# HGRN levels scored in pairs with four level buffers, a resized filler in the last head, and a reordered gate row in the handovers

## The chip, the core and the metric

The kernel runs on one core of one Trainium2 chip. The metric is the device time of one execution in microseconds (us). TensorE (PE in the profile; its weight loads PEld), VectorE (DVE), ScalarE (ACT), GpSimd (POOL) and the DMA queues run side by side, each through its own queue in its own order, and wait for each other by semaphores.

## What is computed

The reference is a two-layer backbone block over 512 latent and 256 context tokens of width 1024, in float32. Layer 0 mixes tokens by retention, layer 1 by a bidirectional gated recurrence (HGRN2) with 8 heads of 128 channels; each layer ends in a gated convolutional feed-forward net (FFN). Around each of the four sub-layers stands the same frame, cut here to its core:

```python
h_l = h_l + g1_l * rms_norm(y_l, norm_g[i, 1])                    # residual, gate row times norm
u_l = rms_norm(h_l, norm_g[i, 2]) * (1.0 + sc2_l) + sh2_l         # input of the next sub-layer
# HGRN2, one head and direction: S_t = diag(a_t) S_{t-1} + k_t v_t^T,  o_t = S_t^T q_t
scores = einsum('bgtk,bgrtsk,bgsk->bgrts', qc, dec, kc)           # dec: product of the gates between s and t
```

## The kernel before

**Order.** TensorE's order is the order in which the program is written (line 1356), except inside the four sub-layer ends, where a small planner writes it. The order on ACT, DVE and POOL is chosen when the program is built, by a scheduler that follows data dependencies, free buffers and its own estimate of times; on the chip each queue is then served in that fixed order.

**HGRN (`hgrn`, from line 1098).** For each head `h`, `project` computes gates `A`, keys `K`, queries and the output gate of the *next* head by large matmuls (tile `hp`, 512 or 256 columns), and `vpart` the values (`hv`). `attend` (line 1168) does the recurrence of the present head in blocks of 128 tokens. Inside a block it doubles the span level by level: for level `li` (0 to 6), ACT copies half of `K` and POOL half of `Q` into a buffer `L` (lines 1201, 1202; three buffers), then DVE multiplies the other halves of `K` and `Q` by the gate totals of this level (line 1208). TensorE forms the scores of the level by `hl`, eight products of 128 x 64 by 128 x 64 (line 1215; sixteen records in the profile), into a PSUM tile of `sml`, of which there are two, and DVE places them by mask into `DG` (line 1219, two instructions). A diagonal `hd` (line 1188), of the same form, stands ahead of level 0. Then follow transposes `ht`, states `hc` and `S`, the output `ho` and its norm `hn`.

**Weaving.** `attend` gives up the floor at every `yield n`. `weave` (line 1285) then lets the filler generator run until it has issued `quota * acc / 37` matmul columns, `acc` being the sum of the yields so far. For heads 0 to 6 the filler is the projection of the next head. For head 7 it is `out1` (line 1266): eight outputs of four chunks, a chunk being three matmuls of 512 columns (`hwo`), which is 8 x 4 x 1536 = 49152 columns, and one step of a side task (`ada`) counted as 4096. Its quota is 64000.

**Sub-layer ends (`tail`, line 515; `handover`, line 392).** A sub-layer's last product is cut into parts of one 128-token block and 512 columns (`tl`). `norms` adds to the plan for each block: two DVE additions out of PSUM (L421), two ACT squares (L424), the factor (L428, L142 to L144), two DVE products of the result with the gate row (L439), one DVE instruction that multiplies by the factor and adds the residual (L450) and the store of the new residual by POOL's DMA queue, then ACT squares (L452), a second factor and the scaling by it, half on DVE (L457), half on ACT (L459). `turn` transposes pairs of blocks on TensorE (L473), modulates (L482) and splits them (L489, L490) into the `u` that the next sub-layer's first products `ld` read. The planner (`Plan.run`, line 49) steps a clock with the costs written in the code; of the ready steps of an engine it emits the one of lowest rank. Transposes have rank 0, the `ld` pieces (24 matmuls each) rank 2, and a transpose counts as ready 0.8 us after its last input. Names of the sub-layer ends: `m0` and `e0` (six blocks, layer 0), `m1` (four blocks, after HGRN), `e1` (the end of the kernel, which has no next sub-layer).

Of the kernel before, what the change touches and what calls it, by code (L numbers as in the profile page):

```python
# [13 lines left out]
ALU = mybir.AluOpType  # L14

P = 128
D = 1024
NF = 8
TL = 512
# [19 lines left out]
class Plan:  # L39
# [5 lines left out]
    def add(self, eng, cost, deps, rank, emit, slack=0.0):  # L45
        self.steps.append(Step(eng, cost, list(deps), rank, emit, slack))
        return self.steps[-1]
# [22 lines left out]
class Net:  # L70
# [321 lines left out]
    def handover(self, nm, y, hsrc, gain, mods, u, hdst, nb, big, tmp):  # L392
        nc = self.nc
        per = y[0].shape[1]
        hx = [big([P, 3, D], F32, f"hx{nm}{j}") for j in range((nb + 2) // 3)]
        if nb % 3:
            g = hx[-1][:, 2:3]
        else:
            g = big([P, 3, D], F32, "gr" + nm)[:, 0:2]
        small = lambda n, w: self.cp.tile([P, w], F32, tag=f"sm{w}", name=f"{n}{nm}", bufs=12)  # L400
        rows = hsrc.rearrange("(b p) d -> p b d", p=P)
        for j, x in enumerate(hx):
            n = min(3, nb - 3 * j)
# [3 lines left out]
        yb = lambda b: y[b // per][:, b % per]  # L407
        hb = lambda b: hx[b // 3][:, b % 3]
# [3 lines left out]
        def norms(b, tails):  # L412
            ts, v, pr = slice(b * P, b * P + P), int(b >= 4), b // 2
            ss, r, q = {}, {}, {}
            add = self.plan.add
            half = lambda c: slice(c * 512, c * 512 + 512)

            def evac(c):
                if not c:
                    ss[0] = small(f"ss{b}", 4)  # L420
                nc.vector.tensor_tensor(yb(b)[:, half(c)], tails[c].ps, yb(b)[:, half(c)], ALU.add)  # L421

            def square(c):
                nc.scalar.activation(tmp(f"sq{nm}{b}{c}"), yb(b)[:, half(c)], AF.Square, accum_out=ss[0][:, c : c + 1])  # L424

            def start(d, x):
                d[0] = small(f"{'rq'[d is q]}{b}", 2)
                nc.scalar.activation(d[0][:, 0:1], x, AF.Abs_reciprocal_sqrt, bias=self.eps, scale=1.0 / D)  # L428

            sq = []  # L430
            for c in range(2):
                e = add("DVE", 0.67, [tails[c]], (pr, 0), lambda c=c: evac(c))
                tails[c].freed = e
                sq.append(add("ACT", 0.75, [e], (pr, 1), lambda c=c: square(c)))
            n = add("DVE", 0.16, sq, (-1,), lambda: nc.vector.tensor_tensor(ss[0][:, 2:3], ss[0][:, 0:1], ss[0][:, 1:2],
                                                                            ALU.add))
            n = add("ACT", 0.28, [n], (-1,), lambda: start(r, ss[0][:, 2:3]))
            n = add("DVE", 0.55, [n], (-1,), lambda: self.newton(r[0], ss[0][:, 2:3]))
            yg = [add("DVE", 0.69, [sq[c]], (pr, 1), lambda cs=half(c): nc.vector.tensor_tensor(  # L439
                yb(b)[:, cs], yb(b)[:, cs], g[:, v, cs], ALU.mult)) for c in range(2)]  # L440
            if u is None:
                for c in range(2):
                    cs = half(c)
                    n = add("DVE", 0.75, [n, yg[c]], (pr, 2), lambda cs=cs: (
                        nc.vector.scalar_tensor_tensor(hb(b)[:, cs], yb(b)[:, cs], r[0][:, 0:1], hb(b)[:, cs],
                                                       ALU.mult, ALU.add),
                        nc.sync.dma_start(hdst[ts, cs], hb(b)[:, cs])))
                return None
            n = add("DVE", 1.28, [n, *yg], (pr, 2), lambda: (
                nc.vector.scalar_tensor_tensor(hb(b), yb(b), r[0][:, 0:1], hb(b), ALU.mult, ALU.add),  # L450
                nc.gpsimd.dma_start(hdst[ts], hb(b))))
            n = add("ACT", 1.23, [n], (pr, 3), lambda: nc.scalar.activation(yb(b), hb(b), AF.Square,  # L452
                                                                           accum_out=ss[0][:, 3:4]))
            n = add("ACT", 0.28, [n], (-1,), lambda: start(q, ss[0][:, 3:4]))
            n = add("DVE", 0.55, [n], (-1,), lambda: self.newton(q[0], ss[0][:, 3:4]))

            return [add("DVE", 0.65, [n], (pr, 3), lambda: nc.vector.tensor_scalar(  # L457
                        yb(b)[:, half(0)], hb(b)[:, half(0)], q[0][:, 0:1], None, ALU.mult)),
                    add("ACT", 0.65, [n], (pr, 3), lambda: nc.scalar.activation(  # L459
                        yb(b)[:, half(1)], hb(b)[:, half(1)], AF.Copy, scale=q[0][:, 0:1]))]  # L460
# [640 lines left out]
    def hgrn(self, outs0, u, mk, nxt):  # L1101
        nc, t, tc = self.nc, self.t, self.tc
# [5 lines left out]
        ip = ies.enter_context(tc.tile_pool(name="heads", bufs=1))  # L1108
        tl = lambda shape, tag, name, bufs: ip.tile(shape, F32, tag=tag, name=name, bufs=bufs)
        tmp = lambda n, w=TL: hp.tile([P, TL], F32, tag="t", name=n, bufs=8)[:, :w]  # L1110
        mf = tl([P, 7, P], "L", "mf", 3)
        nc.scalar.dma_start(mf, t["masks"])
        masks = hp.tile([P, 7, P], U8, name="masks")
        nc.vector.tensor_copy(masks, mf)
        ident = self.ident
        half = lambda n: hp.tile([P, 4, TL], F32, tag="og", name=n, bufs=2)
        og = [half(f"hog{j}") for j in range(2)]
        y, gh, vs = [], [], {}
        ck = lambda x, n: x[:, n * P : n * P + P]
        n4 = lambda x: x.rearrange("p (n l) -> p n l", l=P)  # L1120
# [47 lines left out]
        def attend(h, z):  # L1168
            A, K, q, g = z["A"], z["K"], z["q"], z["g"]
            v = lambda n: vs[h - h % 2][1][n][:, (h % 2) * P : (h % 2) * P + P]  # L1170
            k0 = tmp(f"k0{h}")
# [4 lines left out]
            for li in range(7):  # L1176
# [3 lines left out]
                nc.gpsimd.tensor_tensor(nt, pr[:, :, :, 0], pr[:, :, :, 1], ALU.mult)  # L1180
                tots.append(nt)
                cur = nt
            yield 4
            ps = self.sml(f"hd{h}")
            for n in range(4):
                for b in range(2):
                    rows = slice(64 * b, 64 * b + 64)
                    nc.tensor.matmul(ck(ps, n)[rows, rows], ck(k0, n)[:, rows], ck(q, n)[:, rows],
                                     start=True, stop=True, tile_position=(0, 64 * b))
            DG = tl([P, 4, P], "DG", f"DG{h}", 1)  # L1190
            for b in range(2):
                rows = slice(64 * b, 64 * b + 64)
                nc.vector.tensor_tensor(DG[rows, :, rows], n4(ps)[rows, :, rows],
                                        ident[rows, rows].unsqueeze(1).broadcast_to([64, 4, 64]), ALU.mult)
            for li in range(7):
                hh = 1 << li
                vw = lambda x: x.rearrange("p (n l) -> p n l", l=2 * hh)
                hf = (slice(0, hh), slice(hh, 2 * hh))
                L = tl([P, 2, TL], "L", f"L{h}{li}", 3)
                for d in range(2):  # L1200
                    nc.scalar.activation(vw(L[:, 0])[:, :, hf[d]], vw(K[:, d, LAT])[:, :, hf[d]], AF.Copy)
                    nc.gpsimd.tensor_scalar(vw(L[:, 1])[:, :, hf[1 - d]], vw(Q[:, d])[:, :, hf[1 - d]], 1.0, 0.0,  # L1202
                                            ALU.mult, ALU.add)
                tt = tots[li].rearrange("p d (n l) -> p d n l", l=2)
                for X, d, hd in ((K, 0, 0), (K, 1, 1), (Q, 0, 1), (Q, 1, 0)):
                    nb = X.shape[2] // (2 * hh)
                    xv = vw(X[:, d])[:, :, hf[hd]]
                    nc.vector.tensor_tensor(xv, xv, tt[:, d, :nb, 1 - hd : 2 - hd].broadcast_to([P, nb, hh]), ALU.mult)
                yield 3
                ps = self.sml(f"hl{h}{li}")  # L1210
                x = int(li == 6)
                for n in range(4):
                    for b in range(2):
                        rows, cols = (slice(64 * z, 64 * z + 64) for z in (b, b ^ x))
                        nc.tensor.matmul(ck(ps, n)[rows, cols], ck(L[:, 0], n)[:, rows], ck(L[:, 1], n)[:, cols],  # L1215
                                         start=True, stop=True, tile_position=(0, 64 * b))
                for b in range(2):
                    rows, cols = (slice(64 * z, 64 * z + 64) for z in (b, b ^ x))
                    nc.vector.copy_predicated(DG[rows, :, cols],
                                              masks[rows, li, cols].unsqueeze(1).broadcast_to([64, 4, 64]),  # L1220
                                              n4(ps)[rows, :, cols])
            tot = tots[7]
            order = ((4, 5, 0, 1, 2, 3), (5, 4, 3, 2, 1, 0))
            KT = tl([P, 2, 5, P], "KT", f"KT{h}", 1)
# [76 lines left out]
        z = {}  # L1301
        for _ in chain(project(0, z, outs0), vpart(0, range(3))):
            pass
        for h in range(NF):
            zn = {}
            if h == 7:
                work, quota = out1(), 64000
            elif h % 2:
                work = project(h + 1, zn, None, vpart(h + 1, range(3)))
                quota = 83000  # L1310
            else:
                work = project(h + 1, zn, None, vpart(h, range(3, 6)))
                quota = 83000
            weave(attend(h, z), quota, 37, work)
            z = zn
# [118 lines left out]
```

## Time and profile before

| | us |
|---|---|
| median of 3 runs | 2145.89 (2145.05 to 2146.91) |
| profiled execution, its own time | 2144.12 |
| span of the profiled execution | 2142.4 |

The span starts with the first instruction of the program and ends with the last. Retention fills the span to about 679 us, the first FFN from there to about 1253, HGRN from about 1288 to 1731, the second FFN the rest; the sub-layer ends lie between. A row of a timeline gives start, duration, engine, line, operation, output and inputs, shapes and the number of merged instructions, and in brackets the engine's idle time ahead of it with what ended it. A matmul's printed duration holds its latency, so starts, not durations, tell its rate.

### The profile page before, as it was taken

The numbers are of one execution on the slowest core, as the hardware profiler recorded it, in microseconds if no ns is written. First come the engines' busy times: TensorE is split into PE (matmuls) and PEld (weight loads), VectorE is DVE, ScalarE is ACT, GpSimd is POOL, SyncE is SP. The second block draws the span as 40 slices with busy tenths as digits, with TensorE's granted clock in tenths as the row PEclk, the third lists the DMA queues.
The fourth block names the chain that finished last, engine by engine and source line by source line (L and its number), as shares of the span: only waits on it lengthen the run. The fifth ranks groups of instructions, "written<-read, shape, count | busy, mean of one in ns | idle before, by whom it ended". The sixth has DMA issues, their size and how long they took to land.

```text
span 2142.4 us, 30771 instructions
## 1 busy us (share of the span) xinstructions
PE 2098.6 (98%) x12288; PEld 1770.1 (83%) x12288; DVE 1344.5 (63%) x2560; ACT 839.4 (39%) x1623; POOL 287.8 (13%) x367
## 2 busy tenths in 40 slices
PE   6999999999999999999999999999999989999998
PEld 4888888888888988788888889888888778888886
DVE  6866565663623677477677566778787864434445
ACT  5542342423613733323122147444444454333323
POOL 3622040220100000000000002333333200000000
PEclk9999999999999999999999999999999989999999
DMA  9122313234133233333333533212121243322233
GB/s 301 40 79 87 120 40 128 79 98 149 50 108 118 91 118 99 119 119 109 128 100 127 188 99 108 60 41 60 40 60 41 79 158 131 99 99 97 85 101 120
DMA packets 186608, 218.24 MB, mean 102 GB/s; under 512 B 6112, under 2 KB 157664, under 8 KB 185696
## 3 DMA queue, kind: packets, MB, share of 16 engines
q1 hardware_dynamic: 180432, 198.90, 28.6%
q0 software_dynamic: 2736, 13.11, 1.6%
q10 hardware_dynamic: 3296, 4.26, 0.6%
q8 instruction: 97, 1.59, 0.3%
q14 instruction: 47, 0.39, 0.1%
HBM read 200.90 MB, written 15.34 MB: 101 GB/s over the span
## 4 chain that ended last, share of the span: by engine, by line
PE 92%; DVE 4%; ACT 2%; DMA 1%; issue 0%; POOL 0%; SPq 0%; DVEq 0%
PE f L121 26%; PE f L1059 12%; PE hp L121 8%; PE v L817 6%; PE tl L526 5%; PE wo L985 5%; PE ld L121 4%; PE g_l L121 4%; PE av L868 3%; PE hv L121 3%; PE qk_l L121 3%; PE g_c L121 2%; PE s L121 2%; PE hl L1215 2%; PE qk_c L121 2%; PE hwo L121 1%
## 5 line engine op out<-in xcount | busy, mean ns | idle before, releaser
L121 PE MATMUL f<-um,hua 128*128 128x512 f32 (+1 forms) x960 | 258.3, 357 | 0.0
L121 PE MATMUL f<-um,huv 128*128 128x512 f32 (+1 forms) x960 | 255.8, 354 | 0.0
L264 DVE SCALAR_TENSOR_TENSOR rows<-rada,sc,rows 128x256 f32<-128x256 f32 x504 | 231.8, 485 | 5.4
L1059 PE MATMUL f<-hd,gt 128*128 128x512 f32 x720 | 228.2, 396 | 0.0
L121 PEld LDWEIGHTS f<-um,hua 128*128 128x128 f32 x960 | 169.5, 189 | 29.7 <-issue 4.4
L121 PEld LDWEIGHTS f<-um,huv 128*128 128x128 f32 x960 | 170.0, 189 | 25.2
L121 PE MATMUL hp<-ue,hhw 128*128 128x512 f32 (+1 forms) x672 | 190.8, 371 | 0.0
L121 PE MATMUL f<-um,lua 128*128 128x512 f32 (+1 forms) x480 | 170.1, 354 | 0.0
L121 PE MATMUL f<-um,luv 128*128 128x512 f32 (+1 forms) x480 | 169.7, 354 | 0.0
L1059 PEld LDWEIGHTS f<-hd,gt 128*128 128x128 f32 x720 | 134.9, 187 | 33.6 <-issue 0.8
L1059 PE MATMUL f<-ld,gt 128*128 128x512 f32 x360 | 142.2, 395 | 0.0
L121 PEld LDWEIGHTS hp<-ue,hhw 128*128 128x128 f32 x672 | 113.0, 189 | 17.5 <-issue 1.4
L121 PE MATMUL hp<-ue,lhw 128*128 128x512 f32 (+1 forms) x336 | 120.2, 358 | 0.4
L817 PE MATMUL v<-hv,ua 128*128 128x512 f32 x384 | 120.5, 390 | 0.0
L121 PEld LDWEIGHTS f<-um,lua 128*128 128x128 f32 x480 | 90.7, 189 | 13.0
L121 PEld LDWEIGHTS f<-um,luv 128*128 128x128 f32 x480 | 90.7, 189 | 12.7
L1031 DVE TENSOR_TENSOR c<-f,c 128x512 f32<-128x512 f32 (+1 forms) x60 | 36.1, 602 | 98.3 <-PE f L121 98.3
L1202 POOL TENSOR_SCALAR L<-Q 128x256 f32<-128x256 f32 x112 | 59.6, 545 | 221.3 <-DVE Q L1174 125.2
L985 PE MATMUL wo<-hwo,ogr 128*128 128x512 f32 x288 | 89.3, 391 | 0.0
L1018 ACT ACTIVATE c<-f,c_conv_b,c_conv_w 128x512 f32<-128x512 f32 (+1 forms) x60 | 42.1, 703 | 113.9 <-PE f L121 113.9
L817 PEld LDWEIGHTS v<-hv,ua 128*128 128x128 f32 x384 | 72.1, 188 | 15.4 <-issue 0.6
L93 ACT ACTIVATE hua<-rua 128x512 fp32r<-128x512 f32 x80 | 44.2, 620 | 100.4 <-DMA rua<-ffn_w_up 53.9
(502 smaller groups left out, 4753.3 us busy)
## 6 DMA issues: line engine op xcount, KB each, us to landing
rada<-ada_w SPq DMA_DIRECT2D x48, 1024.0 KB
rua<-ffn_w_up SPq DMA_DIRECT2D x20, 1024.0 KB
ruv<-ffn_w_up SPq DMA_DIRECT2D x20, 1024.0 KB
rd<-ffn_w_down SPq DMA_DIRECT2D x24, 768.0 KB
rhw<-hg_w_in SPq DMA_DIRECT2D x28, 512.0 KB
rv<-ret_w_in SPq DMA_DIRECT2D x8, 1024.0 KB
rg<-ret_w_in SPq DMA_DIRECT2D x8, 1024.0 KB
rqk<-ret_w_in SPq DMA_DIRECT2D x6, 1024.0 KB
```

The source lines that it names most:

```text
L93: self.nc.scalar.activation(hi, raw, AF.Copy)
L121: nc.tensor.matmul(o, a, b[:, s], start=(i == 0), stop=(i == n - 1))
L264: nc.vector.scalar_tensor_tensor(rows[:, v], raw[:, k], a, rows[:, v], ALU.mult, ALU.add)
L526: self.nc.tensor.matmul(step.ps, l, r[:, k], start=(k == 0 and z == 0), stop=(k == 3 and z == 2))
L817: nc.tensor.matmul(ps, a, b, start=(c == 0 and k == 0 and z == 0), stop=(c == 1 and k == 3 and z == 2))
L868: nc.tensor.matmul(av[width][d], a[:, s, ds], b, start=(first and z == 0), stop=(last and z == 2))
L985: nc.tensor.matmul(ps, l, r[:, k], start=(h == 0 and k == 0 and z == 0), stop=(h == 2 and k == 3 and z == 2))
L1018: nc.scalar.activation(c[:, s], ps, AF.Identity, bias=cb[:, i, mt : mt + 1], scale=w(1))
L1031: nc.vector.tensor_tensor(c[:, s], ps, c[:, s], ALU.mult)
L1059: nc.tensor.matmul(ps, l, r[:, k], start=(k1 + k == 0 and z == 0), stop=(k1 + k == nt - 1 and z == 2))
L1202: nc.gpsimd.tensor_scalar(vw(L[:, 1])[:, :, hf[1 - d]], vw(Q[:, d])[:, :, hf[1 - d]], 1.0, 0.0, ALU.mult, ALU.add)
L1215: nc.tensor.matmul(ck(ps, n)[rows, cols], ck(L[:, 0], n)[:, rows], ck(L[:, 1], n)[:, cols], start=True, stop=True, tile_position=(0, 64 * b))
```

## The change

Three edits.

1. **Levels in pairs.** `attend` is cut into `prepare` (buffer, copies, multiplications), `cells` (the eight products) and `place`. Level 0 is prepared ahead of the first yield, which becomes 7, and its products follow those of the diagonal directly. Levels 1 and 2, 3 and 4, 5 and 6 are prepared together, then one `yield 6`, then the products of both, then both placements. The level buffers become four.
2. **Filler of head 7.** Its quota becomes 53248 (49152 + 4096).
3. **Gate row.** In the three sub-layer ends that have a successor, the two products with the gate row (0.69 each in the plan) are gone; the factor and the gate row are applied in one instruction (1.28), and a separate addition of the residual (1.23) follows, with the store behind it. `e1` keeps its form.

```diff
-            yg = [add("DVE", 0.69, [sq[c]], (pr, 1), lambda cs=half(c): nc.vector.tensor_tensor(
-                yb(b)[:, cs], yb(b)[:, cs], g[:, v, cs], ALU.mult)) for c in range(2)]
             if u is None:
+                yg = [add("DVE", 0.69, [sq[c]], (pr, 1), lambda cs=half(c): nc.vector.tensor_tensor(
+                    yb(b)[:, cs], yb(b)[:, cs], g[:, v, cs], ALU.mult)) for c in range(2)]
...
-            n = add("DVE", 1.28, [n, *yg], (pr, 2), lambda: (
-                nc.vector.scalar_tensor_tensor(hb(b), yb(b), r[0][:, 0:1], hb(b), ALU.mult, ALU.add),
-                nc.gpsimd.dma_start(hdst[ts], hb(b))))
+            n = add("DVE", 1.28, [n], (pr, 2), lambda: nc.vector.scalar_tensor_tensor(
+                yb(b), yb(b), r[0][:, 0:1], g[:, v], ALU.mult, ALU.mult))
+            n = add("DVE", 1.23, [n], (pr, 2), lambda: (
+                nc.vector.tensor_tensor(hb(b), hb(b), yb(b), ALU.add), nc.gpsimd.dma_start(hdst[ts], hb(b))))
...
-        mf = tl([P, 7, P], "L", "mf", 3)
+        mf = tl([P, 7, P], "L", "mf", 4)
...
-            yield 4
-            ps = self.sml(f"hd{h}")
...
-            for li in range(7):
+            def prepare(li):
...
-                L = tl([P, 2, TL], "L", f"L{h}{li}", 3)
+                L = tl([P, 2, TL], "L", f"L{h}{li}", 4)
...
-                yield 3
+                return L
+
+            def cells(li, L):
                 ps = self.sml(f"hl{h}{li}")
...
+                return li, ps
+
+            def place(li, ps):
...
+            L = prepare(0)
+            yield 7
+            ps = self.sml(f"hd{h}")
...
+            done = cells(0, L)
...
+            place(*done)
+            for l0 in (1, 3, 5):
+                Ls = [prepare(li) for li in (l0, l0 + 1)]
+                yield 6
+                for done in [cells(l0 + z, Ls[z]) for z in range(2)]:
+                    place(*done)
...
             if h == 7:
-                work, quota = out1(), 64000
+                work, quota = out1(), 53248
```

## Rows read from the trace of the kernel before

**Rows 1.** The page, parts 1 and 4: TensorE's share; the chain by engine.
```profile
PE 2098.6 (98%) x12288; PEld 1770.1 (83%) x12288; DVE 1344.5 (63%) x2560; ACT 839.4 (39%) x1623; POOL 287.8 (13%) x367
...
PE 92%; DVE 4%; ACT 2%; DMA 1%; issue 0%; POOL 0%; SPq 0%; DVEq 0%
```

**Rows 2.** TensorE's timeline around level 0 of head 0; last two rows: later windows.
```profile
1339.90 0.40 PE L121 MATMUL hp<-ue,hhw 128*128 128x256 f32 x2
1340.14 0.28 PE L121 MATMUL hp<-ue,lhw 128*128 128x256 f32 x1
1340.35 0.69 PE L1215 MATMUL hl<-L 128*64 128x64 f32 x16
...
1341.31 0.28 PE L121 MATMUL hp<-ue,lhw 128*128 128x256 f32 x1
...
1340.46 0.58 PE L1215 MATMUL hl<-L 128*64 128x64 f32 x14
...
1340.81 0.23 PE L1215 MATMUL hl<-L 128*64 128x64 f32 x2
```

**Rows 3.** TensorE's timeline around the states `hc`, heads 2 and 7.
```profile
1470.77 0.39 PE L121 MATMUL hp<-ue,lhw 128*128 128x512 f32 x1
1471.00 1.05 PE L1238 MATMUL hc<-hv,KT 128*128 128x128 f32 x8
...
1472.35 0.39 PE L121 MATMUL hp<-ue,lhw 128*128 128x512 f32 x1
1472.58 0.62 PE L121 MATMUL hp<-ue,hhw 128*128 128x512 f32 x2
...
1719.23 1.95 PE L1238 MATMUL hc<-hv,KT 128*128 128x128 f32 x16
```

**Rows 4.** Timeline of head 3: ACT's copies for level 1, and its products.
```profile
1489.40 0.91 ACT L1201 ACTIVATE L<-AK 128x256 f32<-128x256 f32 x2 [3.28 <-DVE AK L1208]
...
1494.70 0.69 PE L1215 MATMUL hl<-L 128*64 128x64 f32 x16
```

**Rows 5.** Timeline of head 1: levels 4 and 6 on TensorE, DVE between them.
```profile
1405.94 0.69 PE L1215 MATMUL hl<-L 128*64 128x64 f32 x16
...
1414.00 0.69 PE L1215 MATMUL hl<-L 128*64 128x64 f32 x16
...
1407.30 5.03 DVE L94 TENSOR_TENSOR lhw<-rhw,hhw 128x512 fp32r<-128x512 f32 x4
1412.36 1.88 DVE L1219 COPY_PREDICATED DG<-masks,hl 64x256 f32<-64x256 uint8 x4
```

**Rows 6.** Head 7, by stretch (start:end, length, busy, PEclk); longest waits; the side task.
```profile
1687.26:1692.69 5.43, 2.97 (x26) 2.19 (x26) 5.38 (x12) 2.44 (x5) 0.81 (x2) 1.00 0.56 193
1692.69:1713.92 21.23, 21.23 (x173) 15.64 (x173) 20.70 (x43) 9.15 (x21) 4.52 (x8) 0.92 0.16 51
1713.92:1730.55 16.63, 12.20 (x88) 10.74 (x85) 6.56 (x17) 5.23 (x10) 0.00 (x0) 0.90 0.41 130
...
PE hc L1238 <- DVE S L1246: 3.3, 1, 3.3
PE hl L1215 <- DVE DG L1193: 2.5, 1, 2.5
...
1712.91 1.07 PE L216 MATMUL ada<-rada,sc 128*32 128x256 f32 x16
```

**Rows 7.** Timeline of the end `m0`: the last block on DVE, its transposes, `ld`.
```profile
729.30 1.28 DVE L450 SCALAR_TENSOR_TENSOR hxm<-yr,r5m,hxm 128x1024 f32<-128x1024 f32 x1
...
732.70 0.49 DVE L457 TENSOR_SCALAR yr<-hxm,q5m 128x512 f32<-128x512 f32 x1
...
734.66 1.04 PE L473 MATMUL trm<-c_ident,yr 128*128 128x128 f32 x8
...
742.27 0.38 PE L121 MATMUL ld<-um,hfl 128*128 128x256 f32 x1 [0.34 <-DVE um L490]
```

**Rows 8.** Timeline of the end `m1`: ACT, first pair of blocks.
```profile
1748.78 2.20 ACT L583 ACTIVATE hfl<-rfl 128x512 fp32r<-128x512 f32 x4 [2.71 <-PE tl L526]
1750.88 1.04 ACT L452 ACTIVATE yh<-hxm 128x1024 f32<-128x1024 f32 x1
```

More of the change, by code (lines that the diff above doesn't have):

```diff
@@ L1182, in attend @@
                 cur = nt
-            yield 4
-            ps = self.sml(f"hd{h}")
[L1185 to L1189, printed above, removed]
-            DG = tl([P, 4, P], "DG", f"DG{h}", 1)
[L1191 to L1194, printed above, removed]
-            for li in range(7):
+            DG = tl([P, 4, P], "DG", f"DG{h}", 1)
+            def prepare(li):
                 hh = 1 << li
@@ L1216, in attend @@
                                          start=True, stop=True, tile_position=(0, 64 * b))
+                return li, ps
+            def place(li, ps):
+                x = int(li == 6)
                 for b in range(2):
@@ L1221, in attend @@
                                               n4(ps)[rows, :, cols])
+            L = prepare(0)
+            yield 7
+            ps = self.sml(f"hd{h}")
+            for n in range(4):
+                for b in range(2):
+                    rows = slice(64 * b, 64 * b + 64)
+                    nc.tensor.matmul(ck(ps, n)[rows, rows], ck(k0, n)[:, rows], ck(q, n)[:, rows],
+                                     start=True, stop=True, tile_position=(0, 64 * b))
+            done = cells(0, L)
+            for b in range(2):
+                rows = slice(64 * b, 64 * b + 64)
+                nc.vector.tensor_tensor(DG[rows, :, rows], n4(ps)[rows, :, rows],
+                                        ident[rows, rows].unsqueeze(1).broadcast_to([64, 4, 64]), ALU.mult)
+            place(*done)
[4 more added lines that the diff above has]
+                    place(*done)
             tot = tots[7]
```

## Prediction

> **What bounds the kernel now.** I read the page first. TensorE is busy for 98% of the span and carries 92% of the chain that ended last [rows 1]. The reader is to see there that only what shortens TensorE's own queue, or its waits, can move the time; work taken from DVE, ACT or POOL counts only where TensorE waits for it. Then I read TensorE's waits by stretch. In heads 0 to 6 of HGRN they are next to nothing. In head 7 they are large: two of them make 5.8 us [rows 6]. In the sub-layer ends there are a few us each. So edit 1 has to be priced as TensorE's own work in heads 0 to 6, edit 2 as waits in head 7, and edit 3 as waits in `m0`, `e0` and `m1`. Last I read the timelines of these places.
>
> **Edit 1: what a group of small products costs.** Take level 0 of head 0 [rows 2]. The 256-column matmuls around it start 0.12 us apart (1339.90 to 1340.14 for two). The one at 1341.31 is the third after that of 1340.14, so without the group it would have started at 1340.14 + 3 x 0.12 = 1340.50. The group costs 1341.31 - 1340.50 = 0.81 us. Inside it twelve of the sixteen records start between 1340.46 and 1340.81, which is 0.029 us each, so sixteen are worth 0.47. The other 0.81 - 0.47 = 0.34 us are paid once per group, in getting in and out. Is that the price of any group, or of this form? The states `hc` answer: sixteen of them start 0.11 us apart ((1.95 - 0.28)/15, with about 0.28 for the latency of the last). Eight between matmuls of 512 columns, which start 0.23 apart, push the third matmul from 1470.77 + 0.69 = 1471.46 to 1472.35, by 0.89 = 8 x 0.11 [rows 3]. They pay nothing for the change. So the 0.34 belongs to the products of 64 columns, and two such groups in a row should pay it once.
>
> The Trainium skill, "TensorEngine Tiling (Array Packing)", Key Properties, says that changing the tiling mode drains the engine while changing the tile does not; that is the reading which the two rows favour. Against the edit speaks "TensorE: Matmul & The Clock Gate" of the Trainium skill, section "Back-to-back issue gap": with hardware decode off a matmul of 64 columns or fewer costs about 62 ns of issue, and a merged group would then save nothing. Sixteen at 62 ns would be 0.99 us, more than the 0.81 that the whole group takes here, so that condition does not hold in this trace. With the floor of about 25 ns that the same section gives, the estimate for the part paid once would be 0.41 instead of 0.34.
>
> Each of the 8 heads has seven levels and a diagonal, 8 such groups. They become 4 per head. Heads 0 to 6 thus lose 7 x 4 = 28 changes: 28 x 0.34 = **-9.5 us**, wholly on TensorE's path.
>
> **What edit 1 makes TensorE wait for.** Two things must now be ready together, the level buffers and both `sml` tiles. Buffers: level 1 of head 3 has the smallest margin of heads 0 to 6, copies done at 1490.31 for products at 1494.70, 4.4 us [rows 4]. With four buffers nothing is prepared later, and in columns of filler no level but the first of a pair moves, and that one later. I price this at nothing, under cover of those 4.4 us. PSUM: level 6 needs the tile that level 4's placement frees, level 5 that of level 3. In head 1 DVE does 5.03 us of weight splitting ahead of the placements, and four placements, 1.88 us, end at 1414.24 against level 6 at 1414.00; the first two of them, level 4's, end at 1413.3 [rows 5]. Between the end of level 4 and level 6 lie 1414.00 - 1405.94 - 0.62 = 7.4 us, and without level 5 between them 6.6. If DVE keeps the splitting ahead of both placements of a pair, it needs 5.03 + 1.88 and some 0.8 of multiplications, 7.7 us, 1.1 more than there is; level 5's own 0.47 runs in that time, and TensorE would wait about 0.6 us. If it doesn't, nothing. With all multiplications of the next pair ahead as well (eight, some 3.9 us) it would be 10.8 and the wait 4 us. The rows are nearest to the middle case, with the splitting ahead of one placement only and 0.7 us to spare (1414.00 against 1413.3). I take 0.1 per head, **+0.7**, with bounds 0 and +28 (7 x 4).
>
> **Edit 2, head 7.** By the quotas, before: 8 chunks stand ahead of level 0, and 28 chunks and `ada` ahead of level 6; the filler is used up two steps later, and the states run bare. After: 7 chunks ahead of the first group, then 6, 5 and 6, so 24 ahead of levels 5 and 6; then 1, 1 and 2 ahead of the three transposes, `ada` and no chunk ahead of the first state, 0, 1, 1, 2 for the rest. Four chunks (4 x 3 x 0.23 = 2.7 us) and `ada` (1.07, about 1 us of the stream) move behind level 6. DVE is full in the first two stretches (5.38 of 5.43, 20.70 of 21.23) and idle for more than half of the third (6.56 of 16.63) [rows 6]. So up to level 6 TensorE only waits in place of the chunks that left: the gain there is at most the 1 us of `ada` that stood directly ahead of it. In the third stretch the moved 3.7 us fill the waits, 16.63 - 12.20 = 4.4 us; the 3.3 at `hc` also falls because no weights can be split on DVE between the states now (their buffer comes free with the last chunk). PEclk of 0.90 over 16.63 us means some 3.3 us at the lower level, 1.2 GHz, after TensorE's wait; that is 1.7 us of work, lost or not as the new waits fall. The same late split is a new load in `m1`'s start: four ACT splits (2.20 together [rows 8]) and four on DVE beside the last head's norm, up to 1 us. Sum: -1 (before level 6) - 1.7 (clock) - 0.3 (rest of the waits) + 0.5 = **-2.5**, bounds -6 (all 5.8 us of waits gone) and 0.
>
> **Edit 3, the sub-layer ends.** On DVE a block gives up two gate products of 512 columns and gains one addition of 1024. The trace has no such addition there; the nearest row is L450 with 1.28 [rows 7], of the same width and with two tensors from SBUF, and I take 1.2. Total work is about even, but the products ran beside the squares, and the addition stands in the chain: +1.2 us for a block whose chain ends last. In `m0` that is the last block: its half scaled on DVE is done at 733.19, the transposes start at 734.66 [rows 7], 1.47 later, at the end of an `ld` piece. So +1.2 is covered by 0.3 if the order on TensorE stays. But the planner calls the transposes ready 0.8 after their input, so by its rule the margin is 0.67, below 1.2, and they would go behind the next piece (24 x 0.12 = 2.9 us). Then the pieces left cannot cover the second half of the chain, and `ld` at 742.27 comes about 2 us later (2.9 less what ACT makes up by running all four modulations back to back). `e0` shows the same pattern with the same 1.47. I take the later place at two in three: **+1.35 each, +2.7**, bounds 0 and +2.9 each. In `m1` ACT is idle for 2.7 us ahead of 1748.78 and the squares of the first block come only behind four splits, at 1750.88 [rows 8]. Without gate products DVE reaches that block's residual earlier, so that its squares fit into the idle time: **-0.3**, bounds -1 and +1. The store of the residual and its POOL queue shift by 1.2 us and nobody waits for that.
>
> **Sum.** -9.5 + 0.7 - 2.5 + 2.7 - 0.3 = -8.9. The profiled execution took 2144.12 (span 2142.4), so 2135.2 there; the median stands 1.8 above it, so **2137.0**.
>
> **The rivals.**
> - *Everything hides (A+).* The transposes keep their place, head 7 gains 6: -9.5 - 6 - 0.3 gives 2130. For it: 0.3 us of margin, and 5.8 us of waits. Against: the planner's 0.8, DVE full in head 7.
> - *Pairs wait for PSUM, mildly.* The 0.6 us computed above in every head: 7 x 0.6 - 0.7 = +3.5 on the forecast, and with the late place fully paid 2.6 more: 2140.5 to 2143. For it: rows 5. Against: the placements are older in the program than the splitting.
> - *Slower: pairs wait for PSUM, badly.* The scheduler puts the weight splitting and the multiplications of the next pair ahead of four placements, and TensorE waits 2 us or more per head. It decides from 4 x 0.34 = 1.36 us per head on; at 2.0 it is 14.0, and -8.9 - 0.7 + 14.0 = +4.4 gives 2150.3, at 2.5 it gives 2154. For it: DVE is the fullest engine beside TensorE [rows 1]. Against: in the rows the placements still came in time.
> - *The merge saves nothing.* The 0.34 is then paid per tile of PSUM or per semaphore, not per change of form: +9.5, 2145 to 2147. Against: the states, eight or sixteen, pay nothing [rows 3].
>
> **How the numbers follow.** About 0.2% (4.3 us) is what a measurement of this kernel can tell from no change: faster means below 2141.6, slower above 2150.2. Forecast 0.70, with 2132 to 2141; A+ 0.07; mild waiting 0.11, half of it below 2141.6; no saving 0.07; slower 0.05. Faster 0.70 + 0.07 + 0.05 = 0.82; same 0.06 + 0.07 = 0.13; slower 0.05. For 8 in 10 the range holds the forecast, part of mild waiting and the near end of A+: 2131 to 2142.
>
> **What would show it.** Right: 28 changes fewer, merged groups of 32 records that take about 1.28 us out of the stream where two took 1.62; heads 0 to 6 some 9 us shorter together; TensorE's wait at `hc` in head 7 under 1 us; a longer wait of `ld` at the ends of `m0` and `e0`. Wrong: waits of `hl` or `ht` on L1219 in heads 0 to 6, or a merged group with a hole between its halves; transposes at the old place with no wait; a head 7 that waits at level 5 for longer than the waits that it lost.

## The result, and the profile after

The changed kernel takes 2131.77 us (2128.56 to 2131.78, median of 4 runs) against 2146.07 (2145.05 to 2146.91, 4 runs) on the same chip: ratio 0.9932, 95% interval 0.9918 to 0.9945. The profiled execution took 2131.78, span 2130.1, against a span of 2142.4 before: 12.3 us less in the profile, where the medians give 14.3. By the page TensorE still bounds the kernel, as in [rows 1]; DVE has 6% of the chain instead of 4%.

```profile
PE 2089.7 (98%) x12288; PEld 1769.8 (83%) x12288; DVE 1337.4 (63%) x2544; ACT 837.5 (39%) x1623; POOL 295.2 (14%) x367
...
PE 91%; DVE 6%; ACT 2%; DMA 1%; issue 0%; POOL 0%; SPq 0%; DVEq 0%; ACTq 0%
```

Where the 12.3 us went shows the view of busy time by stretch: start and end, length, busy time of PE, PEld, DVE, ACT and POOL with instructions, the granted clock of TensorE, DMA share, GB/s. The five rows are `m0`, `e0`, heads 0 to 6, head 7 and `m1`, each from TensorE's first to its last matmul of the part. Between `m0` and `e0` and behind `m1` the two kernels agree within 0.1. Before:

```profile
678.35:752.21 73.86, 72.83 (x480) 66.67 (x479) 51.44 (x112) 51.18 (x111) 3.26 (x6) 1.00 0.34 123
1252.77:1323.40 70.63, 68.09 (x432) 61.01 (x432) 49.55 (x109) 52.34 (x114) 3.20 (x6) 1.00 0.34 112
1323.40:1682.20 358.80, 358.00 (x2873) 308.48 (x2872) 279.97 (x508) 154.39 (x323) 129.42 (x177) 1.00 0.19 54
1682.20:1730.55 48.35, 40.87 (x299) 31.58 (x298) 37.18 (x76) 21.86 (x43) 9.12 (x15) 0.93 0.28 89
1730.55:1790.64 60.09, 55.92 (x337) 48.71 (x336) 40.04 (x83) 37.59 (x80) 2.20 (x4) 0.91 0.38 133
```

After:

```profile
677.45:749.83 72.38, 72.38 (x481) 66.60 (x480) 50.99 (x106) 52.12 (x113) 3.25 (x6) 1.00 0.36 128
1250.37:1317.95 67.58, 67.58 (x432) 60.90 (x432) 49.34 (x104) 51.93 (x114) 3.19 (x6) 1.00 0.32 106
1317.95:1670.54 352.59, 351.04 (x2874) 307.60 (x2873) 274.61 (x507) 153.75 (x323) 137.19 (x177) 1.00 0.20 57
1670.54:1716.72 46.18, 40.05 (x299) 31.41 (x298) 34.37 (x72) 19.51 (x39) 9.00 (x15) 0.93 0.22 72
1716.72:1778.30 61.58, 55.77 (x338) 48.97 (x336) 40.68 (x81) 39.46 (x85) 2.20 (x4) 0.89 0.41 145
```

Length minus PE's busy time is PE's waiting. In `m0` and `e0` it falls to nothing (73.86 - 72.83 = 1.0 and 2.5 before), and these parts are 1.5 and 3.1 shorter. Heads 0 to 6 are 6.2 us shorter, but their waiting rises from 0.8 to 1.6. Head 7 is 2.2 shorter, `m1` is 1.5 longer (waiting 4.2, then 5.8). The stretch ahead of `m0`, which no edit touches, is 0.9 shorter; over all profiles here it lies between 0.9 under and 2.95 over that of before, and with it goes TensorE's granted clock there, in shares of 2.4 GHz: 0.993 before, 0.995 after, 0.988 in the longest (e8 below). So the edits are judged by stretch, and the medians only say whether the sum agrees.

**The merged group.** TensorE's timeline in head 0, levels 3 and 4, answers to [rows 2]:

```profile
1348.58 0.28 PE L121 MATMUL hv<-lhv,ue 128*128 128x256 f32 x1
1348.70 0.28 PE L121 MATMUL hv<-hhv,ue 128*128 128x256 f32 x1
1348.91 1.15 PE L1208 MATMUL hl<-L 128*64 128x64 f32 x32
1349.99 0.39 PE L121 MATMUL hv<-hhv,ue 128*128 128x256 f32 x1
1350.21 0.28 PE L121 MATMUL hv<-lhv,ue 128*128 128x256 f32 x1
```

The matmul at 1350.21 is the second after that of 1348.70 and would have stood at 1348.94: the 32 records cost 1.27 us. Two groups of 16 cost 2 x 0.81 = 1.62 before. The switch that is saved, the way into the 64-column form and out of it, is worth the 0.34 of the prediction within 0.01. The same reckoning over all groups of heads 0 to 6 gives 45.9 us for the 56 of before and 39.1 for the 28 of after, of which 28 x 1.274 = 35.7 are the products and 3.4 are waits inside or at the edge of a group (0.7 before).

**The waits of the pairs** lie between the two halves. Timelines of ACT, TensorE and DVE in head 2 (levels 1 and 2), then of TensorE and DVE in head 3 (diagonal and level 0):

```profile
1435.15 0.42 ACT L1192 ACTIVATE L<-AK 128x256 f32<-128x256 f32 x1 [0.38 <-DVE AK L1199]
...
1439.25 0.69 PE L1208 MATMUL hl<-L 128*64 128x64 f32 x16
1440.20 0.69 PE L1208 MATMUL hl<-L 128*64 128x64 f32 x16 [0.26 <-ACT L L1192]
...
1439.60 0.46 DVE L1216 COPY_PREDICATED DG<-masks,hl 64x256 f32<-64x256 uint8 x1
...
1481.46 0.69 PE L1226 MATMUL hd<-qg,k 128*64 128x64 f32 x16
1482.26 0.69 PE L1208 MATMUL hl<-L 128*64 128x64 f32 x16
...
1481.53 0.68 DVE L143 SCALAR_TENSOR_TENSOR whg<-hn,whg 128x512 f32<-128x512 f32 x1
```

The releaser printed for 1440.20 is an ACT copy. But ACT's two copies for level 2 had, by their order, ended by 1435.6 (first row); what ends at 1440.06 is the placement of level 0 on DVE, which still reads the small PSUM tile that level 2 needs. In head 3 level 0 starts after DVE has read `hn`, the tile of the norm of the head before. And the last pair of head 2 meets the case of [rows 5]: DVE has the weight splitting ahead, the four placements begin at 1453.77, and the group at 1455.17 has a hole that makes it 1.40 long instead of 1.15:

```profile
1455.17 1.40 PE L1208 MATMUL hl<-L 128*64 128x64 f32 x32
...
1451.52 2.22 DVE L94 TENSOR_TENSOR lhw<-rhw,hhw 128x512 fp32r<-128x512 f32 x2
1453.77 1.88 DVE L1216 COPY_PREDICATED DG<-masks,hl 64x256 f32<-64x256 uint8 x4
```

**Head 7**, TensorE's waits there (line waiting, releaser, sum, times, longest), answers to [rows 6]: the 3.3 at the states is gone, the wait behind the diagonal has grown from 2.5 to 4.0.

```profile
PE hl L1208 <- DVE DG L1231: 4.0, 1, 4.0
PE hl L1208 <- DVE DG L1216: 1.6, 1, 1.6
```

**The sub-layer ends.** Timelines of `m0`, blocks 4 and 5. The first three rows are DVE and ACT before, then DVE, ACT, DVE and PE after (they answer to [rows 7]):

```profile
712.99 0.69 DVE L421 TENSOR_TENSOR yr<-tl,yr 128x512 f32<-128x512 f32 x1 [0.17 <-PE tl L526]
...
722.92 1.94 ACT L482 ACTIVATE hxm<-trm,mod,mv0A 128x256 f32<-128x256 f32 x4 [0.58 <-PE trm L473]
...
725.77 0.64 ACT L424 ACTIVATE sqm<-yr 128x512 f32<-128x512 f32 x1
```
```profile
717.51 0.68 DVE L421 TENSOR_TENSOR yr<-tl,yr 128x512 f32<-128x512 f32 x1
...
718.63 0.61 ACT L424 ACTIVATE sqm<-yr 128x512 f32<-128x512 f32 x1
...
719.25 0.55 ACT L483 ACTIVATE hxm<-trm,mod,mv0A 128x256 f32<-128x256 f32 x1
...
723.47 1.28 DVE L449 SCALAR_TENSOR_TENSOR yr<-yr,r5m,grm 128x1024 f32<-128x1024 f32 x1
724.78 1.23 DVE L452 TENSOR_TENSOR hxm<-hxm,yr 128x1024 f32<-128x1024 f32 x1
...
728.85 0.48 DVE L458 TENSOR_SCALAR yr<-hxm,q5m 128x512 f32<-128x512 f32 x1
...
730.95 1.03 PE L474 MATMUL trm<-c_ident,yr 128*128 128x128 f32 x8
```

The addition takes 1.23 us and stands in the chain, as forecast. But the chain starts earlier: before, the squares of the last block stood on ACT behind the whole modulation of the pair before it (725.77); now they are done ahead of it (718.63). Before, nothing on DVE kept them back: the last addition out of PSUM for these two blocks ended at 713.68, 12 us ahead of them. They were late by the order in which ACT's queue was written; inside the ends the planner's order holds for ACT and DVE too, not only for TensorE (`manual_schedule` in `tail`). The block is scaled at 729.3 instead of 733.2, and its transposes stand one `ld` piece earlier, not later.

In `m1` it went the other way ([rows 8]): DVE puts four weight splits between the scaling and the addition of block 1, its squares come at 1741.45, and the first transposes wait 4.58 us.

```profile
1736.39 2.50 DVE L588 TENSOR_TENSOR lfl<-rfl,hfl 128x512 fp32r<-128x512 f32 x4
1738.81 1.22 DVE L452 TENSOR_TENSOR hxm<-hxm,yh 128x1024 f32<-128x1024 f32 x1
...
1741.45 1.04 ACT L453 ACTIVATE yh<-hxm 128x1024 f32<-128x1024 f32 x1
...
1745.45 1.73 PE L474 MATMUL trm<-c_ident,yh 128*128 128x128 f32 x7 [4.58 <-DVE ss3m L435]
```

### The profile page after: what moved, and what is told of

It is laid out like the page before. It is cut to its first block, busy times and chain, and to the rows that moved or that the text cites. A ratio compares the mean times of both kernels' runs of the same rounds, so it can differ in the third digit from the quotient of the medians.

```text
span 2130.1 us, 30763 instructions
## 1 busy us (share of the span) xinstructions
PE 2089.7 (98%) x12288; PEld 1769.8 (83%) x12288; DVE 1337.4 (63%) x2544; ACT 837.5 (39%) x1623; POOL 295.2 (14%) x367
## 4 chain that ended last, share of the span: by engine, by line
PE 91%; DVE 6%; ACT 2%; DMA 1%; issue 0%; POOL 0%; SPq 0%; DVEq 0%; ACTq 0%
PE f L121 26%; PE f L1060 12%; PE hp L121 6%; PE v L818 6%; PE tl L527 5%; PE ld L121 5%; PE wo L986 5%; PE g_l L121 4%; PE av L869 4%; PE hv L121 3%; PE qk_l L121 3%; PE g_c L121 2%; PE s L121 2%; PE qk_c L121 2%; PE hl L1208 1%; PE hc L1255 1%
## 5 line engine op out<-in xcount | busy, mean ns | idle before, releaser
L1193 POOL TENSOR_SCALAR L<-Q 128x256 f32<-128x256 f32 x112 | 67.6, 615 | 211.6 <-DVE Q L1175 130.8
L818 PEld LDWEIGHTS v<-hv,ua 128*128 128x128 f32 x384 | 72.1, 188 | 15.3 <-issue 0.6
```

The source lines that it names most:

```text
L818: nc.tensor.matmul(ps, a, b, start=(c == 0 and k == 0 and z == 0), stop=(c == 1 and k == 3 and z == 2))
```

## The experiments

All lengths in us, from the profile of each kernel by the same five stretches; in brackets what TensorE waits in it. The medians are beside the kernel before of the same session, which took 2145.2 (first eight), 2144.1 (the next two) and 2144.7 (the last two).

| kernel | median | ratio, 95% interval | `m0` | `e0` | heads 0-6 | head 7 | `m1` |
|---|---|---|---|---|---|---|---|
| before | | | 73.9 (1.0) | 70.6 (2.5) | 358.8 (0.8) | 48.4 (7.5) | 60.1 (4.2) |
| after | 2131.8 | 0.9918-0.9945 | 72.4 (0) | 67.6 (0) | 352.6 (1.6) | 46.2 (6.1) | 61.6 (5.8) |
| e1 edit 3 alone | 2141.6 | 0.9974-0.9991 | 72.4 (0) | 67.6 (0) | 358.8 (0.8) | 48.9 (9.3) | 60.9 (5.8) |
| e2 edit 1 alone | 2140.2 | 0.9962-0.9982 | 73.9 (1.0) | 72.1 (2.5) | 352.5 (1.6) | 48.7 (9.0) | 57.5 (4.2) |
| e3 edit 2 alone | 2142.3 | 0.9975-0.9993 | 73.9 (1.0) | 70.6 (2.5) | 358.8 (0.8) | 46.5 (5.3) | 59.4 (4.6) |
| e4 one tile | 2128.1 | 0.9910-0.9935 | 72.4 (0) | 67.6 (0) | 348.3 (0.3) | 45.1 (6.5) | 60.8 (5.8) |
| e5 apart | 2136.5 | 0.9947-0.9972 | 72.4 (0) | 67.6 (0) | 357.9 (0.4) | 45.3 (5.0) | 61.1 (6.0) |
| e6 `m1` old | 2130.2 | 0.9914-0.9939 | 72.4 (0) | 67.6 (0) | 352.5 (1.6) | 44.9 (6.4) | 57.5 (4.2) |
| e7 squares first | 2140.3 | 0.9969-0.9986 | 77.7 (2.6) | 73.0 (2.6) | 352.5 (1.6) | 46.1 (5.9) | 59.4 (4.8) |
| e8 one tile, `m1` old | 2126.2 | 0.9896-0.9927 | 72.4 (0) | 67.6 (0) | 348.4 (0.3) | 45.1 (5.1) | 59.7 (3.8) |
| e9 gates late | 2131.5 | 0.9928-0.9955 | 72.3 (0) | 67.6 (0) | 352.5 (1.5) | 45.9 (5.7) | 60.7 (8.0) |
| e10 one tile, gates late | 2127.8 | 0.9913-0.9938 | 72.3 (0) | 67.6 (0) | 348.2 (0.3) | 45.1 (6.5) | 60.7 (7.4) |
| e11 three buffers | 2130.5 | 0.9918-0.9946 | 72.4 (0) | 67.6 (0) | 350.9 (1.0) | 46.1 (6.5) | 61.0 (6.7) |
| e12 e8, more filler ahead | 2126.0 | 0.9900-0.9927 | 72.4 (0) | 67.6 (0) | 348.3 (0.3) | 45.9 (7.4) | 59.1 (4.4) |

**e1, e2, e3: each edit alone.** e1 is the kernel before with the third edit, e2 with the first, e3 with the second (the diff above).

> The kernel before with edit 3 alone. Theory: the trace of the changed kernel shows the last pair's transposes of m0 and e0 one ld piece earlier (behind 72 ld matmuls instead of 96), m0 1.5 us and e0 3.0 us shorter and m1 1.5 us longer, and none of this needs the other edits: 2146.1 - 1.5 - 3.0 + 1.5 = 2143.1, between 2142 and 2144.5. Rival (the prediction's term): the added link costs 1.35 us in each of m0 and e0, and what the changed trace shows there came from the 0.9 us by which that part started earlier: 2147 to 2149.

> The kernel before with edit 1 alone (pairs, four level buffers; quota of head 7 and the sub-layer ends as before). Theory: heads 0 to 6 give 6.2 us (28 switches of 0.34 us less 2.8 us of new waits and some 0.5 not placed), head 7 between 0 and 2: 2138 to 2140. Rival: the waits of the changed kernel come from the changed filler of head 7 or from the sub-layer ends; then heads 0 to 6 give the full 9.5: 2136 or less.

> The kernel before with edit 2 alone (quota 53248 for head 7, single levels). Theory: chunks move behind level 6 and fill the waits of the states, 1 to 3 us less: 2143 to 2145. Rival: with single levels DVE is full in the first two stretches of head 7, TensorE waits there for what it gains behind: 2146 within 1.

The gains stay where they were in the full change: `m0` -1.45 and `e0` -3.06 belong to edit 3 (e1), the 6.3 of heads 0 to 6 to edit 1 (e2), 1.9 of head 7 to edit 2 (e3). So the rival of e1, that the added link costs time in `m0` and `e0`, is out, and e2's rival, that edit 1 alone would give the full 9.5, and e3's, that edit 2 gives nothing, too. The three medians lie 0.2 to 0.7 outside their expected ranges; those of e1 and e3 were counted from the 2146 of the first session, and the kernel before took 0.9 less in this one. In `m1` the waiting of edit 3 (5.8) is that of the full change; with e2 it is as before. That e2's `m1` is still 2.6 shorter and its `e0` 1.5 longer is TensorE's clock: over `m1` the granted clock was 0.97 of 2.4 GHz in e2 and 0.91 before, over `e0` 0.98 and 1.00, with the same waits. By the medians the three give 3.7, 5.0 and 2.9, 11.6 of the 14.3.

**e4: one PSUM tile for each pair.** The second group of a pair goes into the 64-column blocks that the first leaves free.

```diff
-            def cells(li, L):
-                ps = self.sml(f"hl{h}{li}")
-                x = int(li == 6)
+            def cells(li, L, ps, x):
...
-                        rows, cols = (slice(64 * z, 64 * z + 64) for z in (b, b ^ x))
-                        nc.tensor.matmul(ck(ps, n)[rows, cols], ck(L[:, 0], n)[:, rows], ck(L[:, 1], n)[:, cols],
+                        rows, cols, to = (slice(64 * z, 64 * z + 64) for z in (b, b ^ int(li == 6), b ^ x))
+                        nc.tensor.matmul(ck(ps, n)[rows, to], ck(L[:, 0], n)[:, rows], ck(L[:, 1], n)[:, cols],
...
-            done = cells(0, L)
+            done = cells(0, L, ps, 1)
...
-                for done in [cells(l0 + z, Ls[z]) for z in range(2)]:
+                ps = self.sml(f"hl{h}{l0}")
+                for done in [cells(l0 + z, Ls[z], ps, z) for z in range(2)]:
```

> The changed kernel, but both groups of a pair go to one PSUM tile (the second one into the blocks of 64 columns that the first leaves free), so that a pair needs one of the two small tiles instead of both. Theory: the new waits inside merged groups (2.8 us in heads 0 to 6, and 4.05, 0.17 and 1.59 us in head 7) are for a small PSUM tile that DVE has not read yet; with one tile for a pair the 2.8 go and of head 7's at least the 1.6: 2131.8 - 4.4 = 2127.4, between 2125 and 2128.5. Rival: they are for the level buffers and their copies on ACT, as the releasers in the wait list name: 2131 to 2132.

2128.1. In heads 0 to 6 every merged group now takes 1.27 to 1.28 us, and they are 4.3 us shorter than after: the 3.4 in the groups, and 0.9 at the transposes `ht`, which use the same tiles. The row of head 2 that had the wait:

```profile
1440.30 1.15 PE L1206 MATMUL hl<-L 128*64 128x64 f32 x32
```

So the waits were for the PSUM tile, though the list of waits named ACT's copies. In head 7 the theory holds only in part: the wait behind the diagonal goes, but waits for the level copies of the next pairs take its place (6.5 us in all, 6.1 after). DVE is full there: in the changed kernel it is busy for 16.69 of the 17.02 us from 1681.02 to 1698.04.

**e5: the pairs apart.** Everything as after, with one chunk of filler between the halves.

```diff
-            yield 7
+            yield 6
...
+            yield 1
             done = cells(0, L)
...
-                yield 6
-                for done in [cells(l0 + z, Ls[z]) for z in range(2)]:
+                yield 5
+                first = cells(l0, Ls[0])
+                yield 1
+                for done in (first, cells(l0 + 1, Ls[1])):
```

> The changed kernel with its pairs prepared, buffered and placed as it has them, but one chunk of filler (three matmuls) between the two groups of each pair, so that there are again eight groups per head. Theory: each in and out of the 64-column form costs 0.34 us, four more per head in heads 0 to 6 are +9.5, of which up to 2.8 come back because the waits inside pairs fall into the chunk: heads 0 to 6 longer by 6.7 to 9.5, 2138.5 to 2142. Rival (the merge saves nothing, and the gain of edit 1 comes from preparing in pairs with four buffers): 2131 to 2133.

2136.5, 4.7 more than after by the medians, below the expected range; heads 0 to 6 are 5.3 longer. The price of a switch stands: each group of 16 takes 0.81 out of the stream again (TensorE's timeline of head 2: the matmul at 1434.56 would have stood at 1433.39 + 3 x 0.12 = 1433.75), and 28 x 0.34 = 9.5 less the 3.4 + 0.9 that vanish with the waits is 5.2. What was too low in the expectation was the waits that come back. The rival, that the gain came from the preparation in pairs, is out.

```profile
1433.39 0.28 PE L121 MATMUL hp<-ue,lhw 128*128 128x256 f32 x1
1433.60 0.69 PE L1226 MATMUL hd<-qg,k 128*64 128x64 f32 x16
1434.21 0.51 PE L121 MATMUL hp<-ue,hhw 128*128 128x256 f32 x2
1434.56 0.28 PE L121 MATMUL hp<-ue,lhw 128*128 128x256 f32 x1
```

**e6: the old form in `m1` alone.**

```diff
-            if u is None:
+            if u is None or nm == "m1":
                 yg = [add("DVE", 0.69, [sq[c]], (pr, 1), lambda cs=half(c): nc.vector.tensor_tensor(
```

and for `m1` the old line with `[n, *yg]` in place of the two new steps.

> The changed kernel with the old form of the sub-layer end (gate products first, no addition) in m1 alone. Theory: m1 has four blocks and its first pair of transposes comes right behind the last projection; there the addition stands in the chain with no cover, TensorE's waits in m1 were 4.2 us with the old form and 5.8 with the new one, in the kernel with edit 3 alone too: 1.6 us less, 2129 to 2131. Rival: the longer m1 comes from head 7's late weight splitting (edit 2), not from the form: 2131 to 2132.5.

2130.2, and `m1` waits 4.2 again: the 1.6 us is the form's. The rest of the 4 us by which `m1` is shorter in this profile is the clock (0.97 against 0.89).

**e7 and e9: why `m0` and `e0` became shorter.** Both keep the old form of the ends in all three. e7 only ranks the squares ahead of the modulations of the pair before; e9 only ranks the gate products behind the evacuations of the next pair.

```diff
-                sq.append(add("ACT", 0.75, [e], (pr, 1), lambda c=c: square(c)))
+                sq.append(add("ACT", 0.75, [e], (pr - 1, 3), lambda c=c: square(c)))
```
```diff
-            yg = [add("DVE", 0.69, [sq[c]], (pr, 1), lambda cs=half(c): nc.vector.tensor_tensor(
+            yg = [add("DVE", 0.69, [sq[c]], (pr + 1, 0.5), lambda cs=half(c): nc.vector.tensor_tensor(
```

> The changed kernel with the old form of the sub-layer ends in m0, e0 and m1, but with the squares of a pair ranked ahead of the modulations of the pair before it. Theory: what made m0 and e0 shorter is that the last block's squares no longer stand behind a pair's modulations on ACT (717.8 instead of 725.8 in m0), whatever becomes of the gate products; then m0 and e0 have no TensorE wait at their ends with the old form either, m0 about 72.4 and e0 about 67.6 us long. Rival: it is the gate products that hold DVE; then m0 and e0 are as before, 73.9 and 70.6 us.

> The changed kernel with the old form of the sub-layer ends in m0, e0 and m1, but with the gate products of a pair ranked behind the evacuations of the next pair on DVE. Theory: what made m0 and e0 shorter is that the gate products no longer stand on DVE ahead of the last pair's evacuations, so that its squares come early on ACT and its transposes one ld piece earlier; the form (products or an addition) doesn't matter. Then the last pair's transposes stand behind 72 ld matmuls as in the changed kernel, no wait at the ends, m0 72.4 and e0 67.6 us; m1 as with the old form or better, 57.5 to 60 at TensorE's clock of the run: 2129 to 2132. Rival: the addition itself is what helps (hb free for the load or the store later); then m0 73.9 and e0 70.6 us as before, 2135 to 2137.

e7 missed: `m0` is 77.7 and `e0` 73.0, longer than before. The last pair's end has no wait any more. But the planner now writes the sixteen transposes of the second pair in one row, with no `ld` piece between their halves, and TensorE waits there instead, first for the modulations on ACT, then for the parts of `u` (2.6 us in each of the two ends, and 0.98 of the clock):

```profile
718.59 1.04 PE L473 MATMUL trm<-c_ident,yr 128*128 128x128 f32 x8
720.30 0.66 PE L473 MATMUL trm<-c_ident,yr 128*128 128x128 f32 x4 [0.68 <-ACT hxm L482]
```

The modulations themselves start no later than before (719.23 against 719.18). So the early place of the squares is worth something only if the rest of the written order stays as good. e9 shows that it can: without the new form, `m0` is 72.3 and `e0` 67.6, with no wait, and the last rows of `m0` are those of after, squares ahead of the modulations and the transposes behind 72 `ld` matmuls instead of 96:

```profile
720.00 0.61 ACT L424 ACTIVATE sqm<-yr 128x512 f32<-128x512 f32 x1
...
720.61 0.55 ACT L482 ACTIVATE hxm<-trm,mod,mv0A 128x256 f32<-128x256 f32 x1
...
731.91 1.04 PE L473 MATMUL trm<-c_ident,yr 128*128 128x128 f32 x8
```

So what edit 3 did for `m0` and `e0` was to change the order that the planner writes, and another rank for the gate products changes it in the same way; the instructions themselves don't matter. Which of the planner's choices turns on the products, no run shows; e9's own account, that on DVE they stood ahead of the last pair's additions out of PSUM, does not explain it: before, these additions ended 12 us ahead of the last squares. In `m1`, e9 did worse than either form and worse than expected (60.7 for 57.5 to 60): its first transposes wait 6.4 us.

**e8 and e10: both causes together.** e8 is e4 with the old form in `m1`, e10 is e4 with the ends of e9.

> The changed kernel with one PSUM tile for each pair and the old form of the sub-layer end in m1 alone. If both causes are told rightly, their gains add: one tile for a pair gave 3.7 us against the changed kernel, the old form in m1 gives 1.6: 2126.5, between 2125 and 2128. If the end of m1 is bound by what head 7 leaves on DVE and ACT, the second gain is lost and it is 2128.

> The same with one PSUM tile for each pair. If both causes stand: 3.7 to 4.4 us less than with the gate products late alone, 2125 to 2128, no waits inside the merged groups of heads 0 to 6. If the waits of the pairs had hidden something, less than 2 us.

2126.2 and 2127.8: the gains add. e8 is the better end for `m1`, and by the medians 5.6 us under the changed kernel, though each was timed in its own session.

**e11: three level buffers** instead of four, in the changed kernel.

> The changed kernel with three level buffers instead of four. Theory: the buffers are not what the pairs wait for; with three, the second level of a pair is copied only when the pair before it has been read, and of the margins of 4.6 to 5.7 us that the copies of levels 2 and 4 have in heads 1 to 6, most is left: 2131.8, within 1.5. Rival: DVE's multiplications and the copies run one behind the other, a buffer that comes free late shifts the whole row, and the pairs wait 0.3 to 1 us more per head: 2134 to 2139.

2130.5. The fourth buffer is not needed; without it heads 0 to 6 are 1.7 us shorter (350.9), which neither theory had. With three, the multiplications of the next pair come later, and fewer of them stand on DVE ahead of the placements. TensorE and DVE in head 2, levels 1 and 2, then the row of the changed kernel that answers to the last:

```profile
1440.75 1.43 PE L1208 MATMUL hl<-L 128*64 128x64 f32 x32
...
1440.89 0.45 DVE L1216 COPY_PREDICATED DG<-masks,hl 64x256 f32<-64x256 uint8 x1
...
1442.82 0.94 DVE L1216 COPY_PREDICATED DG<-masks,hl 64x256 f32<-64x256 uint8 x2
```
```profile
1442.48 0.93 DVE L1216 COPY_PREDICATED DG<-masks,hl 64x256 f32<-64x256 uint8 x2
```

The placement of level 0 ends 0.6 us behind the group's start, not 0.8, level 1 is placed 1.2 us sooner after its products, and the last pair has no hole. By the reckoning of the merged group the waits in the groups of heads 0 to 6 fall from 3.4 to 1.6 us. The fourth buffer thus made the PSUM waits longer; the two medians, 1.3 us apart and from two sessions, can't show it.

**e12: more filler ahead of level 6 in head 7**, on top of e8 (57000 in place of 53248).

> One PSUM tile for each pair, the old form of the sub-layer end in m1, and 57000 in place of 53248 as the size of head 7's filler, which puts two chunks more (1.4 us of TensorE) ahead of levels 5 and 6 and leaves hn none. Theory: with one tile for a pair TensorE still waits 4.9 us ahead of level 6 in head 7, for level copies behind a full DVE, and none behind it; two chunks more there fill 1.4 us of that: 2126.2 - 1.4 = 2124.8, between 2124 and 2126. Rival: the tail runs bare again, as in the kernel before (3.3 us at the states): 2126 to 2129.

2126.0, no different from e8. The theory fell: TensorE waits more in head 7 (7.4), probably because the stretch up to level 6 is as long as DVE's row there, however much filler TensorE has; the tail did not run bare as the rival had it (0.14 us at the states, 0.7 at `hn`).

## Why the prediction was right or wrong

The total, 2137.0 forecast with 2131 to 2142, came out at 2131.8, near the low end, and its parts were off in both directions. That it stayed inside was in part luck: the PSUM waits came out 2.9 us worse than their term and `m1` 1.8 worse, `m0` and `e0` together 7.3 better, for a reason that the prediction did not have.

| term | forecast | profile |
|---|---|---|
| heads 0 to 6, switches | -9.5 | -9.5 |
| heads 0 to 6, PSUM waits | +0.7 | +3.6 |
| head 7 | -2.5 | -2.2 |
| `m0` | +1.35 | -1.5 |
| `e0` | +1.35 | -3.1 |
| `m1` | -0.3 | +1.5 |
| ahead of `m0`, no edit | 0 | -0.9 |

The +3.6 is worked out: 3.4 - 0.7 in the groups, 0.9 at `ht`; the two first rows then give -5.9, against -6.2 by the length of the stretch. The 0.3 that is left over I have not placed.

- *The price of a switch* was right, and e5 confirms it by putting the switches back. The Trainium skill, "TensorEngine Tiling (Array Packing)", Key Properties, names the drain at a change of mode, and the trace agrees in what it can show: 0.34 us for one in and out, paid once by two adjacent groups; that the engine drains meanwhile, no row shows. The issue cost of 62 ns that its page "TensorE: Matmul & The Clock Gate" gives under "Back-to-back issue gap" for the case without hardware decode is not seen here: 32 records take 1.15 us with the latency of the last, and even a product of two records takes only 0.058.
- *PSUM waits* were the right mechanism with the wrong size: 0.1 us per head was taken, 0.5 came. The step that failed is "the rows are nearest to the middle case": only level 6 behind the weight splitting was worked out, in one head. The same two tiles also serve `hn` ahead of the first pair (0.33 in odd heads), level 0's placement ahead of level 2 (0.45 to 0.5 in even heads) and `ht`. With four buffers the prediction asked only whether something is prepared later; that the next pair's multiplications come earlier and delay the placements (e11) it had as an outer bound alone.
- *The buffers at nothing* was right: ACT's copies are done at least 4.6 us ahead in heads 1 to 6, and three buffers are enough.
- *Head 7* came out at -2.2 for -2.5, and edit 2 alone gives 1.9 (e3), but not by the parts named, so that the size was in part luck. The states' 3.3 is gone as forecast. The largest term, 1.7 for the clock, did not come: the granted clock over head 7 is 0.93 before, after and in e3. And ahead of level 6, where 1 was to be gained, the wait behind the diagonal grew from 2.5 to 4.0, and 1.6 were added inside the last pair. Its four saved switches brought next to nothing there (46.2 with pairs, 46.5 without); that heads 0 to 6 alone were counted was right, and the likely reason is that DVE's row sets the time up to level 6 (e4, e12).
- *The sub-layer ends* were wrong in sign. The cost of the addition was right (1.23 for 1.2), its place in the chain too. The step that failed is "the addition stands in the chain: +1.2 us for a block whose chain ends last": the place where the chain begins, the last block's squares, was taken as given [rows 7]. The row ahead of them, four modulations on ACT, was not read. All cases, the rival *everything hides* included, had the transposes at the old place or later; they went earlier. The rival's 2130 is nearer in time, but for another reason.
- *`m1`* was read from ACT's idle time [rows 8], and block 0 did use it. The addition of block 1, now a step of its own, came behind four weight splits on DVE; the +1 of the bounds was exceeded by the 1.6 of waits.

Of what was to show it wrong, the merged group with a hole between its halves did appear. Of what was to show it right, heads 0 to 6 gave 6.2 us instead of some 9, and the longer waits at the ends of `m0` and `e0` did not come.

## What to carry to other kernels

Before several small groups are merged, list every tile that the merged group must hold at once and who still reads each; a second half that finds free room in the first half's tile had nothing to wait for and gave another 4.3 us here. Where a planner writes the order, a removed step is worth what then moves forward in the queues, so read the rows ahead of the chain on each engine, and don't take the chain's start as given. A wait for several semaphores is labelled with the last event near it: compare that event with the time at which its result was needed, as with ACT's copies here.

## What the runs showed of the hardware

The 0.34 us of a switch is spread over several starts, not one: 0.21 instead of 0.12 from the last matmul of 256 columns into the group, 0.10 instead of 0.05 from the group's first product, which makes two records, to its second (1348.91 to 1349.01), 0.15 out of it where the next product would have come after 0.05, and 0.22 instead of 0.12 between the next two large matmuls (1349.99 to 1350.21). That the cost goes on behind the group was not expected.
